# Moving all expert weight loads to one queue, and shortening a router head and a long-list branch, in a two-block transformer kernel

## The chip, the cores and the metric

The kernel runs on one core of a Trainium2 chip. The metric is the device time of one execution in microseconds (us), the median over several runs. Half of a microsecond matters little here; the kernel is close to two milliseconds long.

## The reference, cut to what matters

T = 256 tokens of D = 1024 features pass through two layers (a token mixer and a grouped mixture of experts each), then through a second block (window attention, convolutional feed-forward, short convolution, feed-forward). The change lies in the mixture of experts and in the statistics ahead of it:

```python
def rmsnorm(x, g):
    y = x * lax.rsqrt(jnp.mean(x * x, axis=-1, keepdims=True) + EPS)
    return y * g

def grouped_moe(h, w_router, router_bias, w_gate, w_up, w_down):
    t = h.reshape(-1, D)
    scores = jax.nn.sigmoid(t @ w_router)
    biased = (scores + router_bias).reshape(-1, N_GROUPS, EXPERTS_PER_GROUP)
    group_score = lax.top_k(biased, 2)[0].sum(-1)
    _, gidx = lax.top_k(group_score, TOPK_GROUPS)          # 1 of 4 groups
    ...
    _, eidx = lax.top_k(masked, TOP_K)                     # 2 of its 4 experts
    ...                                                    # combine: weights that sum to 1
    for e in range(N_EXPERTS):                             # 16
        he = jax.nn.silu(t @ w_gate[e]) * (t @ w_up[e])    # D -> 512
        y = y + combine[:, e:e + 1] * (he @ w_down[e])     # 512 -> D
```

## The kernel before, in words

**Weights.** One expert has 6 MB of float32 weights, read as six loads of 1 MB: gate, up, gate, up, down, down. A layer has 96 such loads. They go into 16 buffers used in turn, so load n + 16 waits until the load n has been used up. `early` issues four during the token mixer's merge, the head issues further ones, and the call `ahead(6 * e + 14 - n)` ahead of expert e keeps the loads up to number 6e + 14 issued. In `ahead` every odd load after the sixth goes to GpSimd's queue (in effect all gate loads and the first down load of each expert); the others, all up loads among them, go to SyncE's queue.

**Head.** `Stats` adds up the squares of x over the features and sums over partitions with matmuls against a 128x128 matrix of ones, which gives the norm's factor as a row repeated on all partitions (`rnorm`, 128x256). After x has been transposed (L1077, 16 transposes into `xps`), four one-column matmuls (L1083) turn the factor into a column by token, and L1085 copies it to `rtok`. From there VectorE and ScalarE work out the logits (L1087), sigmoid, ranks, the mask `mkb` (L1125), the normalised weights `cmb` (L1126 to L1129) and the place of each token in each expert's list, `pos` (L1141). `ht` holds the normalised tokens, split in a rounded part and a rest (L1148, L1149: four pairs of 128x512). `places(0)` makes the one-hot matrix `PG` (L1348) for the first four experts; `gather` (L1168) multiplies `ht` with it, which yields 64 list slots for each of four experts. Ahead of the first gather four matmuls (L1186) zero the accumulator `yT`.

**Experts.** Each expert does gate and up (L1191, L1192: 64 slots by 512), the silu product (L1208, L1209), the table for its way back (L1177 to L1181), then in the `Else` branch scatters expert e-2 (L1275), transposes its own product (`turn`, L1215) and does the down product of expert e-1 (L1234, L1235). Experts 4g + 2 and 4g + 3 also gather for the next four.

**Long lists.** If an expert has over 64 tokens, the `If` branch runs (`beyond`): a one-hot `pg` for the places after 64 (L1288), a gather by matmul (L1294), copies, transposes (L1300), the gain (`gained`, L1159), gate and up with 32 columns (L1201), silu, transposes (L1223), down (L1254), a weighting into `y`, and a scatter (L1275). The down product leaves four quarters of 256 features on four groups of 32 partitions. Three pairs of instructions write `y`: L1258 and L1259 for all quarters, and L1262 and L1263 twice, to move 32 partitions beside their neighbours; `still` zeroes the rows left over on GpSimd. With this input three experts are long: 6 and 7 in layer 0 and 13 in layer 1.

A scheduler orders each engine's instructions by data; the order of the source sets priorities.

Of the kernel before, what the change touches and what calls it, by code (L numbers as in the profile page):

```python
# [108 lines left out]
def tile_kernel(ctx, tc, A, out, dbg=None, stop=None):  # L109
# [100 lines left out]
    lgs = ctile([128, 2, NE], name="lgs")  # L210
    wnorm = ctile([128, 2], name="wnorm")
# [355 lines left out]
    def token_mix(l):  # L567
        key = (0, l)
        with ExitStack() as es:
# [418 lines left out]
            st = Stats(P, lambda: sp.tile([128, T], F32, name=nm("sq"), tag="sq"))  # L988

            lg = P.tile([128, 2, T], F32, name=nm("lg"), tag="o")[:, 0]  # L990
            experts.gn = gain(key, 4, "norm2_g", 8 * l, f"gn2_{l}")
# [4 lines left out]
            for n in range(4):  # L996
                ps = dense2(P, split_w(load_w(A["w_out"][l], 0, 8, 256 * n, 256), hlp, 8), mga, 8)
                for e in range(2):
                    k = 2 * n + e
                    V.scalar_tensor_tensor(xT[:, k], ps[:, e], mod(key, 2, k), xT[:, k], op0=OP.mult, op1=OP.add)  # L1000
                    st.add(k)
# [7 lines left out]
    class Experts:  # L1009
# [32 lines left out]
        def ahead(self, n):  # L1042
            l = self.l
            while n > 0 and self.order:
                e, j, i = self.order.pop(0)
                self.n += 1
                q = nc.gpsimd if self.n > 6 and self.n % 2 and len(self.order) > 5 else None
                if j and e == NE - 1:
                    w = load_w(A["w_down"][l, e], 0, 4, 512 * i, 512, q)
                else:  # L1050
                    w = load_w(A["w_down"][l, e], 256 * i, 2, 0, 1024, q) if j else load_w(A["w_up" if i % 2 else "w_gate"][l, e], 512 * (i // 2), 4, 0, 512, q)
                self.wts.setdefault((e, j), []).append(w)
                n -= 1

    def moe(l, experts):
        key = (0, l)
        with ExitStack() as es:
# [23 lines left out]
            rps = ps_("t")  # L1081
            for t in range(2):
                PE.matmul(rps[:, t:t + 1], rnorm[0:1, 128 * t:128 * t + 128], ones[0:1, 0:1], start=(t == 0), stop=True, skip_group_check=True)  # L1083
            rtok = mp.tile([128, 2], F32, name="rtok")
            V.tensor_copy(rtok, rps[:, 0:2])  # L1085
# [40 lines left out]
            V.tensor_tensor(cmb, mkb, sc_, OP.mult)  # L1126
            V.tensor_reduce(mx[:, 0], cmb, axis=AX.X, op=OP.add)
            V.reciprocal(mx[:, 1], mx[:, 0])
            V.tensor_tensor(cmb, cmb, mx[:, 1][:, :, None].to_broadcast([128, 2, NE]), OP.mult)  # L1129
            dump(f"cmb{l}", cmb)  # L1130
# [10 lines left out]
            V.scalar_tensor_tensor(pos, pc[:, 0:32].rearrange("p (t e) -> p t e", t=2), 1.0, mkb, op0=OP.add, op1=OP.mult)  # L1141
            ht = [mp.tile([128, 2, D], F32R, name=f"ht{i}") for i in range(2)]
# [29 lines left out]
            def scatter_tab(pg, e, pt, w, tag="t"):  # L1172

                pw = sp.tile([128, 2, 2, SL], F32, name=nm("pw"), tag="pw", bufs=1)
                ps = ps_(tag)
                for t in range(2):
                    V.tensor_scalar(pw[:, t], pg(t).bitcast(F32)[:, None, :].to_broadcast([128, 2, SL]), cmb[:, t, e:e + 1], None, op0=OP.mult)  # L1177
# [5 lines left out]
            yT = ps_("yT", (128, KD, T))  # L1183
            for i in range(4):
                zero = chunkb[64:128]
                PE.matmul(yT[:, 2 * i:2 * i + 2].rearrange("p a (b c) -> p (a b) c", c=128), zero, zero[:, None, :].to_broadcast([64, 4, 128]),  # L1186
                          start=True, stop=False, skip_group_check=True)
# [61 lines left out]
            def down_few(he, e, w, y, tag):  # L1249

                py = ps_(tag)
                for j in range(4):
                    for g in range(4):
                        m = PE.matmul(py[32 * g:32 * g + 32, 0:256], he[:, j, 0:SL // 2], cut(e, j, g // 2)[:, 256 * (g % 2):256 * (g % 2) + 256],  # L1254
                                      start=(j == 0), stop=(j == 3), skip_group_check=True)
                    if j == 1:
                        yield m.ins
                S.activation(y[0][:, 0:256], py[:, 0:256], AF.Copy, scale=w)  # L1258
                V.scalar_tensor_tensor(y[1][:, 0:256], py[:, 0:256], w, y[0][:, 0:256].bitcast(F32), op0=OP.mult, op1=OP.subtract)  # L1259
                for a in (0, 64):  # L1260
                    b, r = slice(a + 32, a + 64), slice(a, a + 32)
                    S.activation(y[0][r, 256:512], py[b, 0:256], AF.Copy, scale=w[r])  # L1262
                    V.scalar_tensor_tensor(y[1][r, 256:512], py[b, 0:256], w[r], y[0][r, 256:512].bitcast(F32), op0=OP.mult, op1=OP.subtract)  # L1263
                yield m.ins
# [5 lines left out]
            def scatter(y, pt):  # L1270
                for i in range(2):
                    for k in range(4):
                        for h in range(2):
                            r = slice(64 * h, 64 * h + 64)
                            PE.matmul(yT[:, 4 * h + k], y[i][r, 128 * k:128 * k + 128], pt[r], start=False, stop=False, skip_group_check=True)  # L1275

            def beyond(e, w, level):
# [29 lines left out]
                scatter_tab(lambda t: pg[:, t, 0:SL], e, ptl, wc[:, 1:2])  # L1307
                if level == 1:
                    for r in (32, 96):
                        G.memset(wc[r:r + 32, 1:2], 0.0)  # L1310
# [7 lines left out]
                y = y_  # L1318
                if level == 1:
                    for i in range(2):  # L1320
                        still(y[i])
                for m in (down_few if level == 1 else down)(he, e, wc[:, 1:2], y, "gu"):
                    pass
                scatter(y, ptl)
# [12 lines left out]
            def still(y):  # L1337

                for r in (32, 96):
                    G.tensor_scalar(y[r:r + 32, 256:512].rearrange("p (a b) -> p a b", a=2), ident[r:r + 32, None, :].to_broadcast([32, 2, 128]), 0.0, None, op0=OP.mult)  # L1340

            lists = {}

            def places(g):

                lists[g] = mp.tile([128, 2, 4 * SL], F32R, name=nm("PG"), tag="PG", bufs=1)
                for t in range(2):
                    V.tensor_tensor(lists[g][:, t].rearrange("p (e s) -> p e s", s=SL), slots[:, None, :].to_broadcast([128, 4, SL]),  # L1348
                                    pos[:, t, 4 * g:4 * g + 4, None].to_broadcast([128, 4, SL]), OP.is_equal)
# [7 lines left out]
            places(0)  # L1357
            features(0, range(0, KD, 2))
            for e in range(NE):
# [14 lines left out]
                gate_up(ps, xgs[g], SL * j, w[0], w[1])  # L1374
                x_ = swiglu(ps, "gx")
# [493 lines left out]
```

## Time and profile before

| | |
|---|---|
| median of 3 runs | 1906.54 us (1906.39 to 1906.67) |
| the profiled execution, its own time | 1908.08 us |
| its span in the profile | 1906.1 us |
| mean granted clock of TensorE | 0.969 of full speed |
| TensorE (PE) busy | 1739.3 us, 91% of the span |
| VectorE (DVE), ScalarE (ACT) busy | 1032.4 us, 801.7 us |
| DMA, mean over the span | 245 GB/s, 467.38 MB |

PE is TensorE's matmuls, PEld its weight loads, SP is SyncE, POOL is GpSimd. The profile puts the granted clock beside stretches of time, where 1.00 is 2.4 GHz and 0.50 is 1.2 GHz. "DMA share" is the mean busy share of the core's 16 DMA engines. The first gate matmul of an expert (L1191) marks its start; the 16 experts of layer 0 start between 341.49 and 597.33 us, those of layer 1 between 931.49 and 1181.26 us.

### The profile page before, as it was taken

The page shows a single profiled execution, that of the slowest core. Times are in us where ns is not written, and L with a number is a line of the kernel's source. Part 1 is how long each engine was busy: PE and PEld are TensorE (multiplying, and loading weights), DVE is VectorE, ACT ScalarE, POOL GpSimd, SP SyncE. Part 2 cuts the span into 40 slices and gives each one's busy share as a digit, 9 for nine tenths or more (in the row PEclk, how much of TensorE's full clock was granted, in tenths as well). Part 3 has the DMA queues.
Part 4 walks back from the last instruction along what each step waited for, and adds up shares of the span by engine and source line. Part 5 has one row for each costly group of instructions (what it writes and reads, how often), then busy time and mean ns, then how long its engine had stood idle before and what let it go on. Part 6 is the DMA issues. An engine that isn't in the chain of part 4 may idle for free. (4 is left out here: it accounts for less than half of the span.)

```text
span 1906.1 us, 31042 instructions
## 1 busy us (share of the span) xinstructions
PE 1739.3 (91%) x12551; PEld 1314.8 (69%) x12551; DVE 1032.4 (54%) x1858; ACT 801.7 (42%) x1454; POOL 315.9 (17%) x236
## 2 busy tenths in 40 slices
PE   6989998898989799999798888879899999989998
PEld 4877798434433677789433333766799997979998
DVE  5775555223222886555322122787576676678775
ACT  4544553111111643544211011767465554456663
POOL 1320232111110420224011100130200003440000
PEclk9999999999999899999899999999999999999999
DMA  9777895797799467797699995430388745577520
GB/s 317 249 250 262 295 312 206 267 387 265 273 392 355 147 230 251 264 307 242 223 390 392 393 385 202 161 133 1 118 303 298 254 133 176 178 257 232 190 96 23
DMA packets 263622, 467.38 MB, mean 245 GB/s; under 512 B 9282, under 2 KB 138288, under 8 KB 263392
## 3 DMA queue, kind: packets, MB, share of 16 engines
q1 hardware_dynamic: 239536, 374.68, 56.5%
q0 software_dynamic: 23200, 88.32, 12.1%
q8 instruction: 144, 2.36, 0.5%
q10 hardware_dynamic: 656, 1.32, 0.2%
q14 instruction: 86, 0.70, 0.1%
HBM read 463.24 MB, written 1.05 MB: 244 GB/s over the span
## 5 line engine op out<-in xcount | busy, mean ns | idle before, releaser
L534 PE MATMUL mm<-hh,hi 128*128 128x256 f32 x1584 | 459.6, 290 | 11.1 <-ACT hh L457 5.7
L535 PE MATMUL mm<-hl,hi 128*128 128x256 f32 x1584 | 454.9, 287 | 9.1 <-DVE hl L458 7.5
L536 PE MATMUL mm<-hh,lo 128*128 128x256 f32 x1584 | 454.7, 287 | 4.4 <-DVE lo L516 4.3
L515 ACT CAST hi<-w 128x1024 fp32r<-128x1024 f32 (+4 forms) x330 | 309.7, 971 | 220.5 <-PE mm L535 178.4
L516 DVE TENSOR_TENSOR lo<-w,hi 128x1024 fp32r<-128x1024 f32 (+4 forms) x264 | 302.1, 1157 | 94.7 <-ACT hi L515 94.4
L534 PEld LDWEIGHTS mm<-hh,hi 128*128 128x128 f32 x1584 | 306.6, 194 | 26.2 <-ACT hh L457 8.4
L535 PEld LDWEIGHTS mm<-hl,hi 128*128 128x128 f32 x1584 | 306.7, 194 | 11.9 <-DVE hl L458 7.9
L536 PEld LDWEIGHTS mm<-hh,lo 128*128 128x128 f32 x1584 | 306.5, 193 | 7.8 <-DVE lo L516 5.4
L516 POOL TENSOR_TENSOR lo<-w,hi 128x1024 fp32r<-128x1024 f32 x66 | 167.8, 2547 | 799.3 <-ACT hi L515 799.3
L1191 PE MATMUL ps<-w,xg 128*64 128x512 f32 x512 | 232.0, 606 | 11.4 <-ACT xg L1157 7.0
L1192 PE MATMUL ps<-w,xg 128*64 128x512 f32 x512 | 232.2, 607 | 7.0 <-DMA w<-in_w_up_dram 7.0
L1191 PEld LDWEIGHTS ps<-w,xg 128*64 128x64 f32 x512 | 69.6, 139 | 142.4 <-issue 132.7
L1209 DVE TENSOR_TENSOR gx<-gx,ps 64x512 f32<-64x512 f32 (+1 forms) x35 | 23.4, 669 | 237.4 <-ACT gx L1208 191.4
L1208 ACT ACTIVATE gx<-ps 64x512 f32<-64x512 f32 (+1 forms) x35 | 20.0, 572 | 231.4 <-PE ps L1192 224.4
L1234 PE MATMUL ps<-w,he 128*64 128x512 f32 x240 | 113.1, 608 | 4.2 <-DMA w<-in_w_down_dram 4.2
L1235 PE MATMUL ps<-w,he 128*64 128x512 f32 x240 | 112.4, 606 | 0.1
L369 PE MATMUL ps<-w,crep 128*32 128x512 f32 x768 | 106.1, 605 | 3.2 <-DMA w<-in_ada_w_dram 1.7
L535 PE MATMUL yT<-zl,hi 128*128 128x256 f32 x352 | 99.1, 282 | 0.0
L534 PE MATMUL yT<-zh,hi 128*128 128x256 f32 x352 | 99.1, 281 | 0.0
L536 PE MATMUL yT<-zh,lo 128*128 128x256 f32 x352 | 99.0, 281 | 0.0
L534 PE MATMUL mm<-half,hi 128*128 128x256 f32 x320 | 93.3, 291 | 0.0
L535 PE MATMUL mm<-half,hi 128*128 128x256 f32 x320 | 91.2, 285 | 0.0
(466 smaller groups left out, 3101.4 us busy)
## 6 DMA issues: line engine op xcount, KB each, us to landing
w<-in_ada_w_dram SPq DMA_DIRECT2D x96, 1024.0 KB, 7.0
w<-in_w_up_dram SPq DMA_DIRECT2D x64, 1024.0 KB, 18.8
w<-in_w_gate_dram POOLq DMA_DIRECT2D x56, 1024.0 KB, 13.9
w<-in_ffn_w_up_dram SPq DMA_DIRECT2D x44, 1024.0 KB, 5.4
w<-in_w_in_dram SPq DMA_DIRECT2D x36, 1024.0 KB, 10.3
w<-in_w_down_dram SPq DMA_DIRECT2D x36, 1024.0 KB, 16.6
w<-in_w_down_dram POOLq DMA_DIRECT2D x28, 1024.0 KB, 11.9
w<-in_ffn_w_down_dram SPq DMA_DIRECT2D x22, 1024.0 KB, 5.0
```

Of the source, the lines that this page charges most:

```text
L369: PE.matmul(ps[32 * g:32 * g + 32], crep[blk][:, 4 * s + g, SLOTS - 1 - i:SLOTS + 31 - i], w[i][s][:, g], start=(i + s == 0), stop=(i == n ...
L515: S.copy(hi, raw)
L516: (lo_eng or V).tensor_tensor(lo, raw, hi.bitcast(F32), OP.subtract)
L534: PE.matmul(ps, wh, ah, start=start, stop=False, skip_group_check=True)
L535: PE.matmul(ps, wh, al, start=False, stop=False, skip_group_check=True)
L536: latest[0] = PE.matmul(ps, wl, ah, start=False, stop=stop, skip_group_check=True).ins
L1191: PE.matmul(ps[0:64], xg[:, k, off:off + SL], wg[k // 4][:, k % 4], start=(k == 0), stop=(k == KD - 1), skip_group_check=True)
L1192: m = PE.matmul(ps[64:128], xg[:, k, off:off + SL], wu[k // 4][:, k % 4], start=(k == 0), stop=(k == KD - 1), skip_group_check=True)
L1208: S.activation(x_, ps[0:64], AF.Silu)
L1209: V.tensor_tensor(x_, x_, ps[64:128], OP.mult)
L1234: PE.matmul(py[0:64], he[:, j], cut(e, j, 0), start=(j == 0), stop=(j == 3), skip_group_check=True)
L1235: m = PE.matmul(py[64:128], he[:, j], cut(e, j, 1), start=(j == 0), stop=(j == 3), skip_group_check=True)
```

## The change: what it does

1. `ahead` issues every expert load on SyncE.
2. The norm's factor is summed by token: `squares` multiplies the squares (as the stationary operand) with one column of ones, so that the sums come out by token on partitions, and `rtok` follows by two activations on 128x2. The row `rnorm`, the matmuls L1083 and the copy L1085 are gone.
3. The head: the normalisation of `cmb` stands after `pos`; the second half of the `ht` splits (`rows(1)`) is issued after the first one-hot `PG`; the zeroing of `yT` stands later in the source.
4. Long lists: `gained` alternates ScalarE and VectorE by feature tile, which for the long branch is four and four where all eight were on VectorE; the table is made in four copies of 32 columns (`n=4`), so that `scatter_few` can read the four quarters where they lie; the two pairs L1262 and L1263, `still` and the memset are gone, and the branch has its own `y` tiles.
5. In the branch the scatter of expert e-2 and one quarter of expert e-1's down product stand ahead of the gather, and the rest is spread one quarter at a time.

```diff
+            ssq = P.tile([128, 512], F32, name=nm("ps"), tag="ps")
+            def squares(k):
+                sq = sp.tile([128, T], F32, name=nm("sq"), tag="sq") if k else rnorm
+                after_square(S.activation(sq, xT[:, k], AF.Square))
+                if 0 < k < KD - 2:
+                    V.tensor_tensor(rnorm, rnorm, sq, OP.add)
+                if k >= KD - 3:
+                    for t in range(2):
+                        PE.matmul(ssq[:, t:t + 1], (rnorm if k == KD - 3 else sq)[:, 128 * t:128 * t + 128], ones[:, 0:1], ...)
+                if k == KD - 1:
+                    rstd_of(ssq[:, 0:2], D, rtok)
...
-                q = nc.gpsimd if self.n > 6 and self.n % 2 and len(self.order) > 5 else None
...
-            rps = ps_("t")
-            for t in range(2):
-                PE.matmul(rps[:, t:t + 1], rnorm[0:1, 128 * t:128 * t + 128], ones[0:1, 0:1], ...)
-            V.tensor_copy(rtok, rps[:, 0:2])
...
             V.scalar_tensor_tensor(pos, pc[:, 0:32]..., 1.0, mkb, op0=OP.add, op1=OP.mult)
+            V.tensor_tensor(cmb, mkb, sc_, OP.mult)
+            ...
-            for g in range(2):
+            def rows(g):
                 for t in range(2):
                     S.activation(ht[0][:, t, sl], xps[:, t, sl], AF.Copy, scale=rtok[:, t:t + 1])
                     V.scalar_tensor_tensor(ht[1][:, t, sl], ...)
+            rows(0)
...
-                    if i % 2:
+                    if k % 2:
                         S.activation(dst[:, k], ps[:, i], AF.Identity, ...)
                     else:
                         V.tensor_scalar(dst[:, k], ps[:, i], ...)
...
-                S.activation(y[0][:, 0:256], py[:, 0:256], AF.Copy, scale=w)
-                V.scalar_tensor_tensor(y[1][:, 0:256], ...)
-                for a in (0, 64):
-                    b, r = slice(a + 32, a + 64), slice(a, a + 32)
-                    S.activation(y[0][r, 256:512], py[b, 0:256], AF.Copy, scale=w[r])
-                    V.scalar_tensor_tensor(y[1][r, 256:512], ...)
+                S.activation(y[0], py[:, 0:256], AF.Copy, scale=w)
+                V.scalar_tensor_tensor(y[1], py[:, 0:256], w, y[0].bitcast(F32), op0=OP.mult, op1=OP.subtract)
...
+            def scatter_few(y, pt):
+                for i in range(2):
+                    for k in range(2):
+                        for q in range(4):
+                            r = slice(32 * q, 32 * q + 32)
+                            PE.matmul(yT[:, 2 * q + k], y[i][r, 128 * k:128 * k + 128], pt[r], ...)
...
             places(0)
+            with tc.issue_after(placed[0]):
+                rows(1)
             features(0, range(0, KD, 2))
...
                 gate_up(ps, xgs[g], SL * j, w[0], w[1])
+                if e == 0:
+                    yT = ps_("yT", (128, KD, T))
+                    ...                       # the four zeroing matmuls
...
                     more = beyond(e, w, 1)
+                    place(e - 2)
+                    second((0,))
                     next(more)
-                    place(e - 2)
+                    second((1,))
                     next(more)
                     turn(x_, he[e])
-                    second((0, 1))
+                    second((2,))
                     next(more)
-                    second((2, 3))
+                    second((3,))
                     run(more)
```

**SyncE and GpSimd at the end of layer 0's token mixer.** Before, SyncE's queue held these loads up to the first read of the lists' lengths (`TENSOR_LOAD cnt`); w_3481 is the first load of expert 0.

```order
L162 DMA w_3481<-in_w_gate_dram 128x4x512
L162 DMA w_3483<-in_w_up_dram 128x4x512
L162 DMA w_3487<-in_w_up_dram 128x4x512
L162 DMA w_3491<-in_w_down_dram 128x2x1024
L162 DMA w_3495<-in_w_up_dram 128x4x512
L162 DMA w_3499<-in_w_up_dram 128x4x512
L162 DMA w_3987<-in_w_down_dram 128x2x1024
L1362 TENSOR_LOAD cnt
```

GpSimd's queue held the other loads of the same stretch, between splits of the token mixer's weights.

```order
L162 DMA w_3485<-in_w_gate_dram 128x4x512
...
L162 DMA w_3489<-in_w_down_dram 128x2x1024
...
L162 DMA w_3493<-in_w_gate_dram 128x4x512
L162 DMA w_3497<-in_w_gate_dram 128x4x512
L162 DMA w_3985<-in_w_down_dram 128x2x1024
```

Now all of them stand in SyncE's queue, by their number:

```order
L162 DMA w_3475<-in_w_gate_dram 128x4x512
L162 DMA w_3477<-in_w_up_dram 128x4x512
L162 DMA w_3479<-in_w_gate_dram 128x4x512
L162 DMA w_3481<-in_w_up_dram 128x4x512
L162 DMA w_3483<-in_w_down_dram 128x2x1024
L162 DMA w_3485<-in_w_down_dram 128x2x1024
L162 DMA w_3487<-in_w_gate_dram 128x4x512
L162 DMA w_3489<-in_w_up_dram 128x4x512
L1361 TENSOR_LOAD cnt
L1361 ISA x8
L162 DMA w_3491<-in_w_gate_dram 128x4x512
L162 DMA w_3493<-in_w_up_dram 128x4x512
```

The loads moved from GpSimd to their places by number; the last four loads of this stretch (two of which the rows show) come after the read of the counts.

**VectorE in the head of layer 0.** Before, from the mask `mkb` to the one-hot `PG`; `ht` is a split, the four `rt` and `mx` rows L1126 to L1129 are the weights, L1141 is `pos`.

```order
L1125 TENSOR_TENSOR mkb<-ws 128x32
L1149 SCALAR_TENSOR_TENSOR ht_3375<-ps_3308,rtok,ht_3374 128x512
L1126 TENSOR_TENSOR rt<-mkb,rt 128x32
L1139 CAST cnt<-ps_3365 1x16
L1127 TENSOR_REDUCE mx<-rt 128x2
L1141 SCALAR_TENSOR_TENSOR rt<-ps_3365,mkb 128x32
L1128 RECIPROCAL mx<-mx 128x2
L1129 TENSOR_TENSOR rt<-rt,mx 128x32
L1149 SCALAR_TENSOR_TENSOR ht_3375<-ps_3308,rtok,ht_3374 128x512
L1348 TENSOR_TENSOR PG_3392<-cst,rt 128x256 x2
```

Now, with L1133 the mask, L1144 `pos` and L1345 the one-hot:

```order
L1133 TENSOR_TENSOR mkb<-ws 128x32
L1157 SCALAR_TENSOR_TENSOR ht_3374<-ps_3312,rtok,ht_3373 128x512
L1142 CAST cnt<-ps_3360 1x16
L1144 SCALAR_TENSOR_TENSOR rt<-ps_3360,mkb 128x32
L1145 TENSOR_TENSOR rt<-mkb,rt 128x32
L1146 TENSOR_REDUCE mx<-rt 128x2
L1345 TENSOR_TENSOR PG_3382<-cst,rt 128x256
L1147 RECIPROCAL mx<-mx 128x2
L1345 TENSOR_TENSOR PG_3382<-cst,rt 128x256
L1148 TENSOR_TENSOR rt<-rt,mx 128x32
L1157 SCALAR_TENSOR_TENSOR ht_3374<-ps_3312,rtok,ht_3373 128x512
```

The one-hot now stands ahead of the last two splits and amid the weights, where it stood behind all of them.

**TensorE in a long branch (expert 6 of layer 0; the order is the same in the others).** Before, from the branch on: L1275 is the scatter of expert e-2, L1294 the gather, L1234 and L1235 the down product of expert e-1, L1300 the transposes.

```order
L1275 MATMUL ps_3385<-PT_5716,y_3390 128x256 x2
L1294 MATMUL ps_6834<-ht_3374,pg_6826 128x512
L1294 MATMUL ps_6834<-ht_3375,pg_6826 128x512
...
L1294 MATMUL ps_6840<-ht_3375,pg_6826 128x512
L1275 MATMUL ps_3385<-PT_5716,y_3390 128x256 x6
L1275 MATMUL ps_3385<-PT_5716,y_3391 128x256 x8
L1234 MATMUL ps_6822<-w_6230,he_6274 64x512
L1300 MATMUL ps_6862<-cst,xr_6833 128x128 x4
L1235 MATMUL ps_6822<-w_6230,he_6274 64x512
L1234 MATMUL ps_6822<-w_6230,he_6274 64x512
```

Now L1274 is the scatter, L1300 the gather, L1237 and L1238 the down product, L1306 the transposes.

```order
L1274 MATMUL ps_3513<-PT_5683,y_3380 128x256 x8
L1274 MATMUL ps_3513<-PT_5683,y_3381 128x256 x8
L1237 MATMUL ps_6773<-w_6189,he_6233 64x512
L1238 MATMUL ps_6773<-w_6189,he_6233 64x512
L1300 MATMUL ps_6803<-ht_3373,pg_6795 128x512
L1300 MATMUL ps_6803<-ht_3374,pg_6795 128x512
...
L1300 MATMUL ps_6809<-ht_3374,pg_6795 128x512
L1237 MATMUL ps_6773<-w_6189,he_6233 64x512
L1238 MATMUL ps_6773<-w_6189,he_6233 64x512
L1237 MATMUL ps_6773<-w_6191,he_6233 64x512
...
L1306 MATMUL ps_6817<-cst,xr_6802 128x128 x4
L1238 MATMUL ps_6773<-w_6191,he_6233 64x512
```

Fourteen scatter matmuls and the first quarter of the down product moved from behind the gather to its front.

## Rows read from the trace of the kernel before

**Rows 1.** Windows: us, busy (x count) of each engine, granted clock, DMA share, GB/s.

```profile
341.49:611.50 270.01, 241.82 (x1425) 105.73 (x1424) 64.23 (x156) 39.00 (x88) 34.73 (x49) 0.97 0.88 329
931.49:1203.00 271.51, 234.82 (x1354) 99.59 (x1354) 62.57 (x143) 43.88 (x96) 31.18 (x44) 0.97 0.89 331
971.52:986.97 15.45, 14.36 (x85) 6.58 (x85) 3.38 (x8) 2.47 (x5) 2.21 (x3) 1.00 1.03 389
999.86:1012.70 12.84, 12.39 (x73) 4.89 (x70) 2.77 (x6) 1.75 (x4) 2.22 (x4) 1.00 1.03 390
1012.70:1030.04 17.34, 15.09 (x91) 6.95 (x87) 5.65 (x12) 3.37 (x8) 3.19 (x5) 1.00 1.03 392
564.45:584.49 20.04, 16.44 (x72) 5.69 (x70) 2.78 (x6) 1.75 (x4) 0.00 (x0) 0.83 1.04 393
999.86:1133.13 133.27, 115.28 (x626) 47.94 (x624) 27.64 (x60) 18.22 (x40) 17.98 (x25) 0.97 1.03 390
850.00:875.00 25.00, 25.00 (x210) 23.41 (x209) 12.35 (x15) 14.47 (x19) 10.13 (x4) 1.00 1.00 327
```

**Rows 2.** Waits, layer 1's experts: waiter, what for, total us, times, longest.

```profile
PE ps L1234 <- DMA w<-in_w_down_dram: 4.2, 4, 2.4
PE ps L1192 <- DMA w<-in_w_up_dram: 3.8, 2, 2.5
```

**Rows 3.** DMA queues and issues, 940 to 1131 us, layer 1.

```profile
q0 software_dynamic: 9606, 37.05, 50.5%
q1 hardware_dynamic: 15222, 35.80, 49.9%
...
w<-in_w_gate_dram POOLq DMA_DIRECT2D x25, 1024.0 KB, 14.2
w<-in_w_up_dram SPq DMA_DIRECT2D x24, 1024.0 KB, 24.5
```

**Rows 4.** DMA queues, 575 to 600 us.

```profile
q1 hardware_dynamic: 4061, 9.67, 102.4%
```

**Rows 5.** Timeline, head of layer 0: start, duration, engine, line.

```profile
322.04 0.42 ACT L402 ACTIVATE rnorm<-rnorm 128x256 f32<-128x256 f32 x1
...
322.06 3.63 PE L1077 MATMUL ps<-cst,xT 128*128 128x128 f32 x16 [0.44 <-ACT rnorm L401]
...
326.55 0.38 DVE L1087 SCALAR_TENSOR_TENSOR rt<-lgs,rtok,logit 128x16 f32<-128x16 f32 x2
...
332.52 0.75 DVE L1149 SCALAR_TENSOR_TENSOR ht<-ps,rtok,ht 128x512 fp32r<-128x512 f32 x1
333.19 0.75 DVE L1348 TENSOR_TENSOR PG<-cst,rt 128x256 fp32r<-128x256 f32 x2
333.33 1.86 PE L1186 MATMUL ps<-chunkb 64*128 64x512 bf16 x4 [1.87 <-DVE ht L1149]
...
335.12 3.78 PE L1168 MATMUL ps<-PG,ht 128*128 128x256 f32 x16
```

**Rows 6.** Timeline, head of layer 1.

```profile
913.92 0.42 ACT L402 ACTIVATE rnorm<-rnorm 128x256 f32<-128x256 f32 x1
...
916.15 0.38 DVE L1087 SCALAR_TENSOR_TENSOR rt<-lgs,rtok,logit 128x16 f32<-128x16 f32 x2
...
924.72 3.78 PE L1168 MATMUL ps<-PG,ht 128*128 128x256 f32 x16
```

**Rows 7.** Timeline, long expert 13 of layer 1.

```profile
1142.68 2.13 PE L1294 MATMUL ps<-ht,pg 128*128 128x512 f32 x8 [1.83 <-DVE pg L1288]
...
1154.43 0.38 ACT L1208 ACTIVATE gx<-ps 64x256 f32<-64x256 f32 x1 [2.34 <-issue]
...
1154.84 0.42 DVE L1209 TENSOR_TENSOR gx<-gx,ps 64x256 f32<-64x256 f32 x1 [1.06 <-ACT gx L1208]
...
1159.42 0.48 DVE L1259 SCALAR_TENSOR_TENSOR y<-ps,wc,y 128x256 fp32r<-128x256 f32 x1 [2.65 <-ACT y L1258]
...
1161.45 0.49 DVE L1263 SCALAR_TENSOR_TENSOR y<-ps,wc,y 32x256 fp32r<-32x256 f32 x1 [0.54 <-ACTq L1326]
```

More of the change, by code (lines that the diff above doesn't have):

```diff
@@ L210, in tile_kernel @@
     lgs = ctile([128, 2, NE], name="lgs")
+    rtok = ctile([128, 2], name="rtok")
     wnorm = ctile([128, 2], name="wnorm")
@@ L987, in token_mix @@
             mga = (lambda k: mg_h[k // 2][:, k % 2]), (lambda k: mg_l[k // 2][:, k % 2])
-            st = Stats(P, lambda: sp.tile([128, T], F32, name=nm("sq"), tag="sq"))
             lg = P.tile([128, 2, T], F32, name=nm("lg"), tag="o")[:, 0]
+            ssq = P.tile([128, 512], F32, name=nm("ps"), tag="ps")
[6 more added lines that the diff above has]
+                    for t in range(2):
+                        PE.matmul(ssq[:, t:t + 1], (rnorm if k == KD - 3 else sq)[:, 128 * t:128 * t + 128], ones[:, 0:1],
+                                  start=(k == KD - 3 and t == 0), stop=(k == KD - 1), skip_group_check=True)
+                if k == KD - 1:
+                    rstd_of(ssq[:, 0:2], D, rtok)
             experts.gn = gain(key, 4, "norm2_g", 8 * l, f"gn2_{l}")
@@ L1141, in moe @@
             V.scalar_tensor_tensor(pos, pc[:, 0:32].rearrange("p (t e) -> p t e", t=2), 1.0, mkb, op0=OP.add, op1=OP.mult)
+            V.tensor_tensor(cmb, mkb, sc_, OP.mult)
+            V.tensor_reduce(mx[:, 0], cmb, axis=AX.X, op=OP.add)
+            V.reciprocal(mx[:, 1], mx[:, 0])
+            V.tensor_tensor(cmb, cmb, mx[:, 1][:, :, None].to_broadcast([128, 2, NE]), OP.mult)
+            dump(f"cmb{l}", cmb)
             ht = [mp.tile([128, 2, D], F32R, name=f"ht{i}") for i in range(2)]
             slots = C("slots")
-            for g in range(2):
+            def rows(g):
                 for t in range(2):
@@ L1170, in gather, with scatter_tab @@
                     gained(dst, ps.rearrange("p (k n) -> p k n", n=T), k0, 2)
-            def scatter_tab(pg, e, pt, w, tag="t"):
-                pw = sp.tile([128, 2, 2, SL], F32, name=nm("pw"), tag="pw", bufs=1)
-                ps = ps_(tag)
+            def scatter_tab(pg, e, pt, w, n=2):
+                pw = sp.tile([128, 2, n, 128 // n], F32, name=nm("pw"), tag="pw", bufs=1)
+                ps = ps_("t")
                 for t in range(2):
-                    V.tensor_scalar(pw[:, t], pg(t).bitcast(F32)[:, None, :].to_broadcast([128, 2, SL]), cmb[:, t, e:e + 1], None, op0=OP.mult)
+                    V.tensor_scalar(pw[:, t], pg(t).bitcast(F32)[:, None, :].to_broadcast([128, n, 128 // n]), cmb[:, t, e:e + 1], None, op0=OP.mult)
                     PE.transpose(ps[:, 128 * t:128 * t + 128], pw[:, t].rearrange("p a b -> p (a b)"), ident)
@@ L1181, in scatter_tab @@
                 V.tensor_scalar(pt, ps[:, :T], 0.0, None, op0=OP.is_gt)
[L1183 to L1187, printed above, removed]
             def gate_up(ps, xg, off, wg, wu, ks=range(KD)):
@@ L1306, in beyond @@
                 wc = sp.tile([128, 2], F32, name=nm("wc"), tag="wc", bufs=1)
[L1307 to L1310, printed above, removed]
+                n = 4 if level == 1 else 2
+                scatter_tab(lambda t: pg[:, t, 0:128 // n], e, ptl, wc[:, 1:2], n)
                 yield
@@ L1317, in beyond @@
                 (turn_few if level == 1 else turn)(x_, he)
[L1318 to L1321, printed above, removed]
+                y = [sp.tile([128, 256], F32R, name=nm("yo"), tag=f"yo{i}", bufs=1) for i in range(2)] if level == 1 else y_
                 for m in (down_few if level == 1 else down)(he, e, wc[:, 1:2], y, "gu"):
                     pass
-                scatter(y, ptl)
+                (scatter_few if level == 1 else scatter)(y, ptl)
                 if not last:
@@ L1335, in place @@
                     scatter(y_, tabs[i][0])
-            def still(y):
-                for r in (32, 96):
-                    G.tensor_scalar(y[r:r + 32, 256:512].rearrange("p (a b) -> p a b", a=2), ident[r:r + 32, None, :].to_broadcast([32, 2, 128]), 0.0, None, op0=OP.mult)
             lists = {}
+            placed = [None]
             def places(g):
@@ L1347, in places @@
                 for t in range(2):
-                    V.tensor_tensor(lists[g][:, t].rearrange("p (e s) -> p e s", s=SL), slots[:, None, :].to_broadcast([128, 4, SL]),
-                                    pos[:, t, 4 * g:4 * g + 4, None].to_broadcast([128, 4, SL]), OP.is_equal)
+                    placed[0] = V.tensor_tensor(lists[g][:, t].rearrange("p (e s) -> p e s", s=SL), slots[:, None, :].to_broadcast([128, 4, SL]),
+                                    pos[:, t, 4 * g:4 * g + 4, None].to_broadcast([128, 4, SL]), OP.is_equal).ins
             def features(g, ks):
@@ L1374, in moe @@
                 gate_up(ps, xgs[g], SL * j, w[0], w[1])
+                if e == 0:
+                    yT = ps_("yT", (128, KD, T))
+                    for i in range(4):
+                        zero = chunkb[64:128]
+                        PE.matmul(yT[:, 2 * i:2 * i + 2].rearrange("p a (b c) -> p (a b) c", c=128), zero, zero[:, None, :].to_broadcast([64, 4, 128]),
+                                  start=True, stop=False, skip_group_check=True)
                 x_ = swiglu(ps, "gx")
```

16 lines of the change are left out of this document (4 added, 12 removed).

## The prediction

> **What bounds the kernel now.** I read the windows of the two expert stages first, since nearly all of the change lies there. They take 270.0 and 271.5 us, and in both TensorE is busy for 87 to 90% while the DMA engines are at 0.88 and 0.89 [rows 1]. So two limits lie close together, and the next question is which one ends last in a given expert. An undisturbed expert takes 12.84 us, 17.34 us if it also makes the next lists and half of the gather, and 15.45 us with the other half [rows 1]. The eight experts 5 to 12 of layer 1 (four plain ones, and twice a pair with gathers) would by these take 4 x 12.84 + 2 x 17.34 + 2 x 15.45 = 116.9 us. They took 133.3 us with the DMA at 1.03 and 390 GB/s [rows 1]: **16.4 us are lost**. In layer 0, expert 13 took 20.04 us for 12.84, at a granted clock of 0.83 [rows 1]: **7.2 us lost**.
>
> What is it that comes late? The waits of TensorE for weights in layer 1 name up and down loads and no gate load [rows 2]. The queues show why. In the 191 us from 940 each queue moved about half of the bytes, 37.05 and 35.80 MB, but a gate load on GpSimd's queue landed 14.2 us after its issue and an up load on SyncE's 24.5 us [rows 3]. So the gate weights of a later expert are fetched while the up weights of an earlier one are still waited for, and TensorE needs both. This is a matter of order, not of rate.
>
> The other two places are the heads, in which TensorE waits for a chain on ScalarE and VectorE [rows 5, 6], and the long branch, in which it waits for one-hots and for the weighting [rows 7].
>
> **The change part by part.** The sum is made against the profiled execution's own 1908.1 us, which is 1.5 us over the median of the runs shown, 1906.5; I take the 1.5 off at the end.
>
> *Head.* The factor's second activation ends at 322.46 in layer 0, and the logits start at 326.55, behind 16 transposes (322.06 to 325.69), the small matmuls and a copy [rows 5]. Now the factor comes by token from two activations on two elements, priced at no less than nothing and at most the old 0.42 us [rows 5]; I keep the old time. The logits then start 4.1 us earlier in layer 0, and 916.15 - 914.34 = 1.8 us in layer 1, where the transposes ran faster [rows 6]. A split (0.75 us) that stood just ahead of the one-hot now stands behind it [rows 5]: 0.75 us more, twice. The zeroing (1.86 us) stood between the one-hot's end, 333.94, and the gather at 335.12 [rows 5], so 1.2 us of it was on the path; now it lies amid the gather with its full 1.86, since TensorE has little else there: 0.7 us given back. Sum: -4.1 - 0.75 + 0.7 = **-4.2 us** in layer 0 and **-1.9** in layer 1. Bounds for both: -3, if the first splits must wait for all 16 transposes (until 325.69) and hold the chain on VectorE, where one stands amid the ranks; -9, if the zeroing falls in a wait. The four operations on `cmb` go behind `pos`, in the gather's shade; without that cover they would cost some 0.7 us.
>
> *Long branch, three times.* (a) TensorE idled 1.83 us for the one-hot ahead of the gather [rows 7]. The scatter and a quarter of the down product now stand there; 16 and two matmuls, taken as enough to fill it: -1.8. What is late next is the copy behind the gather, which the other quarters cover. (b) The two extra pairs ran from 1159.90, the end of L1259, to 1161.94, the end of the last L1263, with the scatter's last 11 matmuls behind them [rows 7]. The scatter reads four quarters with as many matmuls as before: -2.0. (c) Before, four pairs of the down product lay ahead of the transposes L1223 and covered the silu product's 0.38 + 0.42 us [rows 7]; now only four transposes do: +0.5, most of that time. (d) Eight gains split over two engines: nothing, since the gate product begins with the first one and follows at its own pace. Sum 3 x -3.3 = **-9.9 us**. Bounds: -6, if (a) is half given back by a later wait, and -14, if fewer waits also keep the clock up.
>
> *Queue.* All loads in one in-order queue land by number, so a gate load no longer passes the up load that goes with it. GpSimd's instructions for the loads are gone; its queue holds nothing else that is waited for. SyncE has five more loads in the head; the read of the counts now stands ahead of the last four, which therefore leave later, for expert 2 onward, some 20 us before use: nothing. What can be recovered is at most what was lost, 7.2 and 16.4 us; the bounds are 0 and -23.6. The transfers set a limit of their own. SyncE alone moved 9.67 MB in 25 us, 387 GB/s, with 102% of the engines' time taken [rows 4], so a load of 1.049 MB takes 2.71 us. The first buffer comes free at about 940, when expert 0 has read its gate weights; the 64 loads from then to the first ones of expert 13 take 64 x 2.71 = 173 us and are there at 1113. By the eight clean experts, expert 13 would start at 999.9 + 116.9 = 1116.8, or 1115 with the head's gain. So the transfers suffice, but with 2 to 3 us to spare where 16.4 are to be won; the down loads have shorter leads and may still be late. I take two thirds: **-11 us** in layer 1, and the **-7.2** of layer 0, whose loss sits in one expert, in full.
>
> By the Trainium skill ("DMA: Bandwidth & Descriptors", section "Issuing engines are not separate DMA queues"), issuing from several engines saves only the sequencer's time, as all DMAs end on the same 16 engines. The rate agrees with it (390 GB/s either way), the 14.2 against 24.5 us to landing does not show such indifference; by that rule alone the queue term would be nothing, which is rival A below.
>
> Sum: -6.1 - 9.9 - 18.2 = -34.2; 1908.1 - 34.2 = 1873.9, and **1872 us** on the footing of the median.
>
> **Rivals.**
> *A, the order is not the cause.* The transfers run at 1.03 through the whole stretch of losses [rows 1]; if they are simply the bound there, who issues them changes nothing. Against it: 173 us of transfers fit before expert 13. It leaves the head and the branches, -16.0: 1892 - 1.5 = 1890.5 us.
> *C, the transfers become the pace.* Order helps until the margin of 2 to 3 us is eaten; then layer 1's head (-1.9) and its long branch (-3.3) buy no time, and only 5 of 16.4 us come back there. -34.2 + 6 + 5.2 = -23: 1885, that is about 1883.5 us.
> *B, the single queue is slower: the other side.* With 2 KB packets from one queue the rate could fall, as in the stretch of 850 to 875, where SyncE's loads alone gave 327 GB/s [rows 1]. Then 64 loads take 64 x 1.049 / 0.327 = 205 us: expert 13 of layer 1 at 1145, 12 us later than its 1133.1, and layer 0, with more slack, 0 to 5 later: with -16.0 elsewhere about no change. It decides below some 320 GB/s; at 300, 224 us, 31 us later in layer 1 and some in layer 0, which gives 1918. Against it: 387 GB/s with SyncE alone on the same kind of loads [rows 4].
> The change does what it says: the order of the loads and of the branch's matmuls is seen in the queues above.
>
> **How the numbers follow.** Forecast 0.62; A 0.18; C 0.10; B 0.07, of which one part in seven ends at no change; other 0.03. A run of this kernel can tell a change from none from about 0.2% on, 3.8 us. Faster: 0.62 + 0.18 + 0.10 + some of the rest = 0.91; same 0.03; slower 0.06. The forecast's own range takes the queue in full and low (-23.6 to -13), the branches -14 to -6 and the head -9 to -3, not all at an end together: 1860 to 1882. The range reaches to A, 1860 to 1892.
>
> **What would show it.** Waits of TensorE for up loads gone or under 2 us in layer 1; SyncE's gate and up loads landing after like times; expert 13 of layer 1 starting 115 to 122 us after expert 5 (133.3 before); expert 13 of layer 0 at 12.8 to 14; the first gather 4 to 6 us nearer to the end of the mixer in layer 0; no gap over 1 us ahead of a long branch's gather. Wrong: the DMA's rate below 350 GB/s in these windows, or a new wait of TensorE on down loads of like size.

## The result and the profile after

The changed kernel takes **1877.3 us** (median of four runs, 1876.0 to 1882.7) against 1906.5 before, a ratio of 0.9854 with a 95% interval of 0.9834 to 0.9874: 29 us faster, where 34 had been forecast (1872). The profiled execution took 1876.0 us, its span is 1874.2, so 31.9 us below the span before. The table divides these 31.9 us at the start of the instruction that writes the last features of x ahead of each head, and at the experts' first gate matmuls (L1191 before, L1194 now).

| stretch | before, us | after, us | difference |
|---|---|---|---|
| start to the last features, layer 0 | 319.6 | 317.9 | -1.6 |
| head of layer 0 | 21.9 | 19.6 | -2.3 |
| layer 0, experts 0 to 14 | 255.8 | 242.1 | -13.8 |
| expert 15 and layer 1's token mixer | 314.1 | 312.9 | -1.2 |
| head of layer 1 | 20.1 | 18.4 | -1.7 |
| layer 1, experts 0 to 14 | 249.8 | 238.0 | -11.7 |
| the rest | 724.9 | 725.3 | +0.4 |

The first row is no gain of the change: TensorE's granted clock over it is 0.98 for 0.97, and in two further profiles of the changed kernel the same stretch takes 319.2 and 322.3 us. These are the windows after, with the columns of [rows 1], for an expert with half a gather (6 of layer 1, [rows 1] has 17.34 us for it), for expert 1 of layer 0, for expert 7 (long) and 13 of layer 0, and for experts 5 to 12, 13 and 14 of layer 1:

```profile
994.28:1011.47 17.19, 15.10 (x91) 6.95 (x87) 5.65 (x12) 3.37 (x8) 0.00 (x0) 1.00 1.04 391
347.35:361.93 14.58, 13.00 (x55) 4.85 (x57) 2.35 (x7) 1.06 (x3) 0.00 (x0) 0.88 0.85 297
452.62:482.00 29.38, 26.32 (x213) 12.58 (x213) 8.68 (x25) 5.92 (x13) 0.00 (x0) 0.99 0.53 194
553.09:566.77 13.68, 12.57 (x72) 5.04 (x70) 2.77 (x6) 1.75 (x4) 0.00 (x0) 1.00 1.04 388
980.67:1097.83 117.16, 108.65 (x627) 46.82 (x625) 27.70 (x60) 18.30 (x40) 0.00 (x0) 1.00 1.04 390
1097.83:1132.57 34.74, 27.25 (x201) 11.45 (x198) 7.78 (x23) 5.89 (x14) 0.00 (x0) 0.90 0.98 369
1132.57:1148.96 16.39, 14.06 (x71) 5.57 (x72) 2.77 (x6) 1.12 (x4) 0.00 (x0) 0.89 0.77 268
```

Experts 5 to 12 of layer 1 lost 16.4 us before [rows 1] and now take 117.2 us, close to the clean sum of 116.9. Layer 0's expert 13 takes 13.7 for 20.0. But expert 13 of layer 1, a long one, takes 34.7 us where it took 32.8. The queue in layer 1 and TensorE's waits for weights from expert 13 on, in the columns of [rows 2, 3]:

```profile
q1 hardware_dynamic: 30399, 71.56, 101.3%
...
w<-in_w_gate_dram SPq DMA_DIRECT2D x24, 1024.0 KB, 15.2
w<-in_w_up_dram SPq DMA_DIRECT2D x23, 1024.0 KB, 16.6
w<-in_w_down_dram SPq DMA_DIRECT2D x22, 1024.0 KB, 14.9
```

```profile
PE ps L1257 <- DMA w<-in_w_down_dram: 3.1, 2, 2.2
...
PE ps L1195 <- DMA w<-in_w_up_dram: 1.6, 1, 1.6
...
PE ps L1237 <- DMA w<-in_w_down_dram: 0.2, 1, 0.2
```

Gate and up loads now land alike after their issue (15.2 and 16.6 us, against 14.2 and 24.5 [rows 3]). The waits of experts 8 to 12 are gone, and in expert 13 new ones stand: one for its up load and, within its branch, two for its down loads. The trace before has no such wait within a branch. The long branch of expert 13 shows them in the timeline, as in [rows 7]:

```profile
1110.49 2.13 PE L1300 MATMUL ps<-ht,pg 128*128 128x512 f32 x8
...
1122.88 0.31 PE L1226 MATMUL ps<-cst,gx 64*128 64x64 f32 x2 [1.06 <-DVE gx L1212]
...
1125.36 1.53 PE L1257 MATMUL ps<-w,heo 128*32 128x256 f32 x16 [2.18 <-DMA w<-in_w_down_dram]
...
1127.84 1.93 PE L1257 MATMUL ps<-w,heo 128*32 128x256 f32 x16 [0.95 <-DMA w<-in_w_down_dram]
...
1130.41 0.48 DVE L1262 SCALAR_TENSOR_TENSOR yo<-ps,wc,yo 128x256 fp32r<-128x256 f32 x1 [6.90 <-ACTq L1327]
...
1130.43 1.32 PE L1281 MATMUL ps<-pto,yo 32*128 32x256 f32 x16 [0.66 <-ACTq L1327]
```

The gather L1300 starts with no idle time of the matmuls ahead of it (1.83 us before), and behind the one pair L1261 and L1262 the scatter L1281 ends it. Between them TensorE waits 1.06 us for the silu product (0.5 had been forecast) and then 2.18 and 0.95 us for weights (the granted clock of the whole expert is 0.90). The head of layer 0, as in [rows 5]:

```profile
320.35 0.20 ACT L403 ACTIVATE rtok<-rtok 128x2 f32<-128x2 f32 x1
...
320.37 3.57 PE L1090 MATMUL ps<-cst,xT 128*128 128x128 f32 x16 [0.35 <-ACT rtok L402]
...
320.58 0.38 DVE L1095 SCALAR_TENSOR_TENSOR rt<-lgs,rtok,logit 128x16 f32<-128x16 f32 x2 [2.18 <-ACT rtok L403]
...
324.04 0.69 ACT L1156 ACTIVATE ht<-ps,rtok 128x512 fp32r<-128x512 f32 x1 [2.07 <-PE ps L1090]
324.76 0.75 DVE L1157 SCALAR_TENSOR_TENSOR ht<-ps,rtok,ht 128x512 fp32r<-128x512 f32 x1 [1.18 <-ACT ht L1156]
...
327.85 0.40 DVE L1345 TENSOR_TENSOR PG<-cst,rt 128x256 fp32r<-128x256 f32 x1
...
328.00 3.75 PE L1177 MATMUL ps<-PG,ht 128*128 128x256 f32 x16 [1.30 <-DVE mx L1147]
...
332.11 1.88 PE L1378 MATMUL ps<-chunkb 64*128 64x512 bf16 x4
...
333.92 3.48 PEld L1177 LDWEIGHTS ps<-PG,ht 128*128 128x128 f32 x16 [0.84 <-ACT xg L1166]
```

The logits start at 320.58, 2.65 us behind the last features (7.0 before), but the first split waits 2.07 us for all 16 transposes, and VectorE's chain waits 1.18 us behind it. The zeroing (1.88 us) stands amid the gather, whose second half waits for ScalarE's gains (L1166) at the same time.

### The profile page after: what moved, and what is told of

It reads as the page before. It is cut to its first block, busy times and chain, and to the rows that moved or that the text cites. A ratio compares the mean times of both kernels' runs of the same rounds, so it can differ in the third digit from the quotient of the medians.

```text
span 1874.2 us, 30827 instructions
## 1 busy us (share of the span) xinstructions
PE 1727.8 (92%) x12555; PEld 1307.8 (70%) x12555; DVE 1026.2 (55%) x1838; ACT 802.4 (43%) x1460; POOL 239.9 (13%) x134
## 5 line engine op out<-in xcount | busy, mean ns | idle before, releaser
L1194 PE MATMUL ps<-w,xg 128*64 128x512 f32 x512 | 231.7, 606 | 8.1 <-ACT xg L1166 5.7
L1194 PEld LDWEIGHTS ps<-w,xg 128*64 128x64 f32 x512 | 69.8, 139 | 149.1 <-issue 138.8
L1238 PE MATMUL ps<-w,he 128*64 128x512 f32 x240 | 110.7, 600 | 0.0
L1237 PE MATMUL ps<-w,he 128*64 128x512 f32 x240 | 110.0, 599 | 0.2 <-DMA w<-in_w_down_dram 0.2
```

What stands on the lines that cost most here:

```text
L1194: PE.matmul(ps[0:64], xg[:, k, off:off + SL], wg[k // 4][:, k % 4], start=(k == 0), stop=(k == KD - 1), skip_group_check=True)
L1237: PE.matmul(py[0:64], he[:, j], cut(e, j, 0), start=(j == 0), stop=(j == 3), skip_group_check=True)
L1238: m = PE.matmul(py[64:128], he[:, j], cut(e, j, 1), start=(j == 0), stop=(j == 3), skip_group_check=True)
```

## The experiments

Experiments 1 to 4, 5 to 8 and 9 to 12 each share a chip and that chip's runs of the kernel before. Lengths of experts are from the one profiled execution of each.

**1. The queue alone.** The kernel before, with

```diff
-                q = nc.gpsimd if self.n > 6 and self.n % 2 and len(self.order) > 5 else None
+                q = None
```

> The kernel before with only the queue rule changed: all expert loads on SyncE. Order theory (a gate load that passes the up load of an earlier expert is the cause of the losses): expert 13 of layer 1 starts 117 to 120 us after expert 5 instead of 133.3, layer 0's expert 13 takes about 13 to 14 us instead of 20.0; in all 18 to 22 us faster than before, 1885 to 1889 us, since the old long branch also hides the late down loads better than the new one does. Rival (the transfers are the bound, whoever issues them): within 4 us of before, 1903 to 1910.

Measured: 1889.9 us, ratio 0.9904 (0.9870 to 0.9937). Layer 0's expert 13 takes 12.85 us, experts 5 to 12 of layer 1 119.6 us, its expert 13 34.8. The rival that the queue is indifferent falls. The gain is a little less than expected; in the profile expert 13 takes 2 us more than before and expert 14 1.3 more. TensorE's waits for weights in these two, which the trace before has none of, are the same kind as in the changed kernel, though the branch (L1254 is its down product) is the old one:

```profile
PE ps L1191 <- DMA w<-in_w_up_dram: 2.9, 1, 2.9
PE ps L1254 <- DMA w<-in_w_down_dram: 2.0, 2, 1.4
```

**2. All but the queue.** The changed kernel with the old rule put back.

> The changed kernel with the old queue rule (odd loads on GpSimd), all else as changed. Order theory: the losses come back, experts 5 to 12 of layer 1 take 130 us or more, time 1890 to 1897 us. Rival (the gain comes from the head and the branches, and the queue is indifferent): 1877 us, as the changed kernel.

Measured: 1885.2 us, ratio 0.9872 (0.9828 to 0.9916): between the two. Experts 5 to 12 of layer 1 take 127.6 us again, less than order alone had led me to expect, and expert 13 then takes only 27.0: what was lost ahead of it is given back there.

**3. One queue, GpSimd's.** `q = nc.gpsimd if self.n > 6 and len(self.order) > 5 else None` in the changed kernel.

> The changed kernel with all expert loads after the sixth of a layer on GpSimd's queue, the last six of a layer on SyncE's: again one queue in order, but the other engine's. Order theory: as good as SyncE's queue within 5 us, 1874 to 1884 us. Rival (SyncE's kind of queue is what helps, GpSimd's is slower or is held up by GpSimd's other work): over 1888 us.

Measured: 1892.0 us, ratio 0.9926 (0.9899 to 0.9952). The order theory missed the time, which is the rival's; but experts 5 to 12 of layer 1 take 117.3 us as with SyncE's queue. Where it lost against the changed kernel is elsewhere: 2.4 to 3.8 us in expert 8 of layer 0, 5 to 7 from the start of its expert 15 to the end of layer 1's token mixer, 3 in expert 13 of layer 1. For expert 15 the timeline of SyncE's queue, the queues from 563 to 590 us and TensorE's waits in layer 0's stage show what happens:

```profile
563.56 1.97 SPq L162 DMA_DIRECT2D w<-in_w_down_dram  x4
581.14 6.30 SPq L162 DMA_DIRECT2D w<-in_ada_w_dram  x2
```

```profile
q1 hardware_dynamic: 2293, 5.57, 54.6%
q0 software_dynamic: 1289, 4.93, 47.4%
```

```profile
PE ps L1196 <- DMA w<-in_w_up_dram: 3.7, 1, 3.7
```

The edit leaves the last six loads of the layer on SyncE's queue, which issues them from 554 us on, and the next layer's loads from 581 on. With these the up load of expert 15, issued at 554.5 us on GpSimd's queue, shared the rate; it landed at 588.7, and TensorE waited 3.7 us for it. That is again two queues out of order. What delayed expert 8 and expert 13 of layer 1 is not settled, so for those the rival stands.

**4. Whole experts on alternate queues.** `q = nc.gpsimd if self.n > 6 and e % 2 and len(self.order) > 5 else None`.

> The changed kernel with the loads of whole experts on alternating queues: odd experts on GpSimd, even ones on SyncE. Order theory: gate and up of an expert now come together, but the next expert's loads share the rate with them, so part of the loss comes back: 1881 to 1892 us, with waits for weights spread over all experts of layer 1. Rival (only a gate and an up load of one expert on two queues hurt): as the changed kernel, 1875 to 1880 us.

Measured: 1891.4 us, ratio 0.9917 (0.9890 to 0.9943). Experts 5 to 12 of layer 1 take 135.1 us, worse than with the old rule. The losses sit in two blocks (expert 8: 20.1, expert 12: 23.6) and are not spread as expected, and the profiled run is the slowest of its six (1899.9 us), so their size is not that of the median. TensorE waits 8.1 us for up loads and 2.7 us for a gate load in layer 1. So it is not the pair of gate and up alone: the loss comes too when the loads that share the rate are those of a later expert.

**5. The changed kernel again.** No edit.

> The changed kernel once more, as the standard for the other three on this chip: 1874 to 1883 us, with layer 1's experts 5 to 12 in 117 us and its expert 13 in 34 to 36 us.

Measured: 1878.2 us, ratio 0.9851 (0.9831 to 0.9871), expert 13 of layer 1 in 34.2 us.

**6. Fewer transfers in layer 1.** The second pair of gate and up weights of experts 6 to 13 is not read.

```diff
                 self.n += 1
+                if l and not j and i > 1 and 6 <= e < 14:
+                    self.wts[e, j].append(self.wts[e, j][i - 2])
+                    n -= 1
+                    continue
```

> The changed kernel, but in layer 1 the experts 6 to 13 do not load the second pair of gate and up weights (16 of 96 loads are left out) and use the first pair in its place, with the same matmuls. Theory (behind expert 12 the transfers are the pace, so that what the branch saves there is lost again): expert 13 of layer 1 takes 29 to 30.5 us in place of 34.7, as the long branches of layer 0, and expert 14 at most 15.5; 5 to 8 us faster than the changed kernel. Rival (the branch's new order itself is slow there): expert 13 stays above 33 us, and the time within 2 us of the changed kernel's.

Measured: 1867.3 us, ratio 0.9784 (0.9762 to 0.9806), 10.9 us below experiment 5, more than expected; between the two profiled executions it is 8.8 us, 8.3 of them in layer 1's experts. Windows of experts 5 to 12, 13 and 14 of layer 1:

```profile
982.77:1099.88 117.11, 108.67 (x626) 46.78 (x624) 27.69 (x60) 18.30 (x40) 0.00 (x0) 1.00 0.91 340
1099.88:1126.95 27.07, 24.12 (x200) 10.73 (x197) 7.78 (x23) 5.91 (x14) 0.00 (x0) 1.00 0.40 153
1126.95:1141.53 14.58, 14.20 (x70) 5.88 (x72) 2.77 (x6) 1.11 (x4) 0.00 (x0) 0.88 0.46 155
```

Experts 5 to 12 take the same 117.1 us, expert 13 takes 27.1 and expert 14 14.6, with TensorE at full clock through the branch and no matmul that waits for weights. The branch's order is not slow; its loads were late.

**7. The branch's old order.** Item 5 of the change undone, all else kept.

```diff
-                    place(e - 2)
-                    second((0,))
                     next(more)
-                    second((1,))
+                    place(e - 2)
                     next(more)
                     turn(x_, he[e])
-                    second((2,))
+                    second((0, 1))
                     next(more)
-                    second((3,))
+                    second((2, 3))
```

> The changed kernel with the old order of scatter, down product and gather in the long branch; the shorter weighting, the split gains and the one queue stay. Theory (the new order fills the wait for the one-hot, 1.8 us, and costs 0.5 us at the silu product): the branches of experts 6 and 7 of layer 0 get 1 to 1.8 us longer each, expert 13 of layer 1 does not, since it waits for loads there; 2 to 4 us slower than the changed kernel. Rival (the shorter weighting and the split gains bring all): within 1 us of the changed kernel.

Measured: 1881.4 us, ratio 0.9855 (0.9837 to 0.9873), by the medians 3.2 us over experiment 5, by the ratios 0.8, and the intervals overlap: the time does not decide between theory and rival. The mechanism shows in the timeline of expert 6 of layer 0, and another thing in expert 7:

```profile
433.16 1.22 PE L1300 MATMUL ps<-ht,pg 128*128 128x512 f32 x2 [1.82 <-DVE pg L1294]
...
468.06 0.58 PE L1274 MATMUL ps<-PT,y 64*128 64x256 f32 x2 [3.53 <-issue]
```

The wait for the one-hot is back (1.82 us), and expert 6 takes 1.3 us more than in experiment 5 (33.8 for 32.5). Expert 7 takes 5.1 us more, of which 3.5 are a stall for which the profile names no releaser, and the granted clock over the expert is 0.90 (0.99 in the changed kernel's profile); that is not the one-hot, and whether it belongs to the order is open (the profiled run is the slowest of its four, 1885.6 us). Expert 13 of layer 1 gets no longer (33.5 for 34.2), as the theory had it.

**8. Zeroing held back** until expert 0's gate and up product (`with tc.issue_after(m.ins)` around the four matmuls).

> The changed kernel with the four zeroing matmuls held back until expert 0's gate and up product, where TensorE waits 1.5 us in both layers. Theory (the zeroing amid the gather costs its full 1.9 us at half clock): both heads get 1.3 to 2 us shorter, and 2.5 to 4 us in all; if the wait behind expert 0 is also what brings the half clock at expert 1 (14.6 us against 12.9), another 1.7 us per layer. Rival (it fell in a wait for the splits or the gains): heads as before, within 1 us of the changed kernel.

Measured: 1876.5 us, ratio 0.9834 (0.9813 to 0.9854). Layer 0's head takes 18.8 us, layer 1's 17.7; the changed kernel itself shows 18.6 to 19.6 and 15.9 to 18.4 in its three profiles, so no gain is seen, as the rival had it. Expert 1 stays at 14.58 us.

**9 to 12. The four corners on one chip, and the zeroing again.**

> The kernel before with only the queue rule changed, beside the other corners of the table on one chip. Floor theory (in layer 1 the transfers set when expert 13 can end, whichever way the waits are spread, so that the queue and the branches partly save the same time): 15 to 20 us faster than before. Additive theory (each part saves its own time): queue and the rest together make the 29 us, so the queue 7 to 9 if the rest saves 20 to 22.

> The changed kernel with the old queue rule. Floor theory: 15 to 24 us faster than before although the queue alone already brings 15 to 20, so that the two savings add to more than the 29 us of both together. Additive theory: 10 to 13 us faster than before (29 less what the queue alone brings).

> The changed kernel as the fourth corner: 28 to 30 us faster than before, by either theory.

> The changed kernel with the zeroing held back until expert 0's gate and up product, a second time. If its first 1.7 us were real: 1 to 3 us faster than the changed kernel of this call. If they were scatter: within 1 us or slower.

| kernel | median, us | ratio to before (95%) |
|---|---|---|
| before | 1905.8 | |
| queue alone | 1889.8 | 0.9922 (0.9907 to 0.9937) |
| all but the queue | 1885.2 | 0.9888 (0.9870 to 0.9907) |
| the changed kernel | 1877.9 | 0.9853 (0.9834 to 0.9872) |
| with the zeroing held back | 1877.3 | 0.9857 (0.9842 to 0.9872) |

By the medians the queue alone saves 16.0 us, the rest alone 20.6, together 28.0 and not 36.6: 8.6 us are saved by either. The additive theory asked for 10 to 13 us from the rest and falls. Held-back zeroing is within scatter; no version that reads all the weights is seen to beat the changed kernel. The intervals leave the 8.6 us uncertain by about 6 (an estimate from the three ratios). The head and the shorter weighting had no run of their own; what they bring is read from the stretches.

One reason why the parts overlap is seen in the time from expert 0's start to the end of expert 13 in layer 1. With one queue on SyncE it is 222.7 and 222.6 us with the old branch and head, 221.6, 220.9 and 221.1 in the changed kernel, 220.4 with the branch's old order, 222.4 and 220.7 with the zeroing held back: **a floor of 220 to 223 us**, whatever the branch does (224.8 with GpSimd's queue). Without 16 of the loads it is 213.7. With two queues and the new branch it is 224.3 and 226.7, before it was 234.4. In the second two-queue run the waits for weights from expert 5 to 14 of layer 1 were these:

```profile
PE ps L1238 <- DMA w<-in_w_down_dram: 5.4, 2, 4.8
...
PE ps L1196 <- DMA w<-in_w_up_dram: 1.5, 1, 1.5
```

They are nearly as large as before [rows 2], but then expert 13 takes 28.0 us, for its own weights have arrived meanwhile.

The other part of the overlap lies in layer 0. There expert 13 takes 20.0 us before and 12.8 with the queue alone, but with two queues and the rest of the change it takes only 15.9 and 13.7: either part removes most of that loss. Experts 0 to 14 of layer 0 get 6.9 and 7.2 us shorter by the queue alone, 9.4 by the rest alone, twice, and 11.2 to 13.8 by both.

## Why the prediction came out as it did

The direction, the range and the cause were right; the sum of 34.2 us was 5 too large by the medians. In the profiled executions it was 2.3 too large (31.9): 4.7 too large in the two heads and in layer 1's experts, against a gain of 2.4 in the other stretches, which is within the scatter of the further profiles.

- **Queue order: right.** Removing the second queue took the loss of experts 5 to 12 away in full (16.1 of 16.4 us; I had taken 11) and 6.4 of the 7.2 us in layer 0. The queue alone gave 14.9 to 18.3 us by its ratios, with 18.2 forecast.
- **The sum over layer 1: the step that failed.** I added the third long branch's -3.3 us to the queue's term, and stopped reckoning the transfers at expert 13's first gate and up loads, "2 to 3 us to spare". The reckoning ought to have gone on through its second pair and its down loads, since the branch reads these too, and layer 1's pace there is the transfers' (experiment 6). The waits come with the queue and not with the branch's new order: experiment 1 has them with the old branch, and the old order (experiment 7) leaves expert 13 at 33.5 us. So what was won ahead of expert 13 and in its branch came back as waits: +2.0 us in expert 13 and +1.0 in 14, where -3.3 was forecast. In layer 1's experts -11.7 us came of -14.3, and 1.7 of the difference is expert 1's clock (below). This is rival C's mechanism. It got a chance of 0.10, with 11.2 us as its price; the order's larger gain paid for most of that. That the layer's sum still came near was luck: the third taken off the queue's 16.4 us had no row behind it, and it covered the branch's loss. One sign that the prediction named as wrong did come: waits for down loads, 3.1 us in the new place (L1257) for 4.2 us before. The rows of SyncE's queue show why these loads were late:

```profile
1100.74 7.61 SPq L162 DMA_DIRECT2D w<-in_w_up_dram  x2
...
1108.45 2.52 SPq L162 DMA_DIRECT2D w<-in_w_gate_dram  x1
...
1111.02 3.79 SPq L162 DMA_DIRECT2D w<-in_w_down_dram  x2
```

The two down loads land at 1125.2 and about 1127.8 us. Ahead of them in the queue stand four gate and up loads of later experts (from 1099.5 us on), some 11 us of transfers at 2.71 us each. The order by number fits an expert whose down product comes one stage later; a long expert needs its own down loads at once. Moving these two ahead was not tried.

- **Rival A** (the bound is the rate, so the queue is indifferent) was wrong for the queue and right on the rate. By the Trainium skill ("DMA: Bandwidth & Descriptors", section "Issuing engines are not separate DMA queues") issuing from several engines saves only the sequencer's time: 390 GB/s from one queue, as from two [rows 1], agree. What decided here is which load comes first; that was worth 15 to 18 us. The same page's section "Queues, rings and completion order" says that the DMA engines take turns between the queues that have work; 36.4 and 34.6 MB from the two queues in the same 189 us of the second two-queue run agree with it. A later load on the one queue then takes rate from an earlier one on the other, as the 14.2 against 24.5 us to landing show [rows 3].
- **Rival B** fell: the single queue moved 390 GB/s. The stretch from 850 to 875 us was no like case: its packets had 1.1 KB in the mean (8.15 MB in 7533), those of the experts' loads 2.4 KB (71.56 MB in 30399), and in part of it little was moved. Its 1918 us does not follow from its terms either; -16.0 and +31 give 1921.5 before layer 0's share.
- **Long branches of layer 0: right**, -3.5 and -3.8 us for -3.3. The wait for the one-hot is gone and returns with the old order (1.82 us); the silu product's exposure was 1.06 and not 0.5 us in each of the three branches.
- **Head of layer 0: the bound, not the value.** -2.3 us for -4.2: the first split waits for all the transposes (2.07 us in the trace) and holds VectorE's chain, the case that I had named as the small bound. The old head with one queue takes 20.5 and 20.9 us (experiments 1 and 9) against 21.9 before, so about 1 us of the gain is the queue's or scatter; no run tells which. Layer 1, whose transposes are done sooner, gave -1.7 for -1.9; in two further profiles of the same kernel it was 15.9 and 16.0 us long, so -4.1; the granted clock over it was 0.89 in these two and 0.72 in the first.
- **The zeroing** cost less than was taken: it lies in a wait of the gather for ScalarE's gains, and holding it back changes nothing that can be told.
- **Not foreseen:** expert 1 is 1.1 and 1.7 us longer in the two layers, at half clock. The four head loads behind the read of the counts cost nothing in time, as said: the buffers were then full anyway. SyncE waits 10.7 us for expert 0's transposes, and the loads go out 8.9 us after expert 0's start, as before. (In the queues above, w_3481 is the first load of expert 1; expert 0's four are the early ones.)

## What to carry to other kernels

When transfers run at full rate and a stage still waits for them, look at the times from issue to landing by kind: unlike ones for loads that are needed together can mean that the order is wrong; here one queue mended it at no cost in rate. Check that the queue's order is the order of need for every path: for the long expert it was not. Then carry the reckoning of the transfers through to the last load of the stretch: behind the first wait that is removed stands the floor of the bytes, and two changes that both shorten the way to that floor do not add. A two by two table of the parts on one chip (neither, each alone, both) shows it in four runs.

## What was not expected of the hardware

- GpSimd's queue alone moved 67.1 MB in the 178 us of layer 1 that I looked at, 377 GB/s at 99.0% of the engines' time, about as SyncE's (71.56 MB in 189 us, 379 GB/s); its instruction takes 0.75 us for a load, SyncE's 0.37 to 0.5 where nothing is ahead of it.
- In every kernel with the new head expert 1 runs partly at half clock (granted 0.88 over the expert in the changed kernel's profile; 14.4 to 16.3 us), in every kernel with the old head it takes 12.9 to 13.5. TensorE idles 1.5 us ahead of the transposes of expert 0; filling about 1 us of that with the zeroing (0.54 us of it were left) did not change it. The cause stays open.
